# RMSNorm and QKV projection on one core: the last 256 columns as one matmul group, copied in halves by two engines, stored once

One core of one Trainium2 chip. The metric is the time of one execution in microseconds (us) on that core, lower is better; most executions of one kernel agree within about 0.3%. TensorE does the matmuls, VectorE (DVE in the profile) and ScalarE (ACT) copy results out of PSUM (the buffer into which TensorE writes), SyncE (SP) issues the stores. A store has landed when it has signalled its semaphore, a counter that other engines can wait for.

## The reference

```python
def setup_inputs():
    batch, n_heads, seq, head_dim = 8, 12, 1024, 64
    dim = n_heads * head_dim                                   # 768
    return {"x": randn(batch, seq, dim), "gamma": ones(dim),
            "w_qkv": randn(dim, 3 * dim) * 0.1, "eps": 1e-5}   # float32

def reference(x, gamma, w_qkv, eps):
    rms = np.sqrt(np.mean(x ** 2, axis=-1, keepdims=True) + eps)
    x_norm = x / rms * gamma
    return np.matmul(x_norm, w_qkv).astype(np.float32)
```

That is a matmul of 8192 x 768 by 768 x 2304. The kernel works in 64 row tiles of 128 rows; a row tile's 2304 output columns are made in groups (512, 512, 512, 512, 256), each of six accumulating bf16 matmuls into one PSUM tile.

## The kernel before

Only the last row tile (t = MT - 1 = 63) matters here. Its last 256 columns are two groups of 128, each in a PSUM tile of its own.

```python
def width(t, n0):
    return P if t == MT - 1 and n0 >= N - 2 * P else min(NT, N - n0)

def mm(t, n0, kos):
    nl = width(t, n0)
    for ko in kos:
        if (t, n0) not in PM:
            PM[t, n0] = psum.tile([P, NT], f32, name="pm")
        ...
        nc.tensor.matmul(out=PM[t, n0][:, :nl], lhsT=XT[t][:, ko, :], rhs=w_b[:, ko, n0:n0 + nl], ...)

def evac(t, n0, eng):
    ...
    if eng == "DVE":
        nc.vector.tensor_scalar(out=o, in0=pm[:, :nl], scalar1=RS[t], scalar2=None, op0=mult)
    else:
        nc.scalar.activation(out=o, in_=pm[:, :nl], func=AF.Copy, scale=RS[t], bias=0.0)

def store(t, h, n0, nl):
    nc.sync.dma_start(out=of[t * P:(t + 1) * P, n0:n0 + nl], in_=OUT[t, h][...])

def evac_at(time, t, n0, eng, gap):
    at(time, evac, t, n0, eng)
    ...
    if t >= MT - 2:                       # the last two row tiles: each group is stored by itself
        at(time + gap - 0.5, store, t, h, n0, nl)
    elif left[t, h] == 0:
        at(time + gap, store, t, h, *PARTS[h])
...
for t in range(HEAD, MT):
    ...                                   # engines alternate from group to group
    for n0 in [*range(0, N, NT)] + [N - P] * (t == MT - 1):
        at(now, mm, t, n0, range(KO))
        now += width(t, n0) * US
        flip ^= 1
        evac_at(now + 0.2, t, n0, "DVE" if flip else "ACT", gap=1.2)
```

Of the kernel before, what the change touches and what calls it, by code (L numbers as in the profile page):

```python
# [92 lines left out]
def kernel(  # L93
# [8 lines left out]
    nc = tc.nc  # L102
    f32 = mybir.dt.float32
    bf16 = mybir.dt.bfloat16
    AF = mybir.ActivationFunctionType
    mult = mybir.AluOpType.mult
# [4 lines left out]
    Kw, N = w_qkv.shape  # L111
    assert K == Kw
    P = 128
    KO = K // P
    MT = M // P
    NT = 512
# [34 lines left out]
    X, XB, XT, RS, OUT, WF, PM, PT = {}, {}, {}, {}, {}, {}, {}, {}  # L151
# [71 lines left out]
    begun = {}  # L223

    def width(t, n0):

        return P if t == MT - 1 and n0 >= N - 2 * P else min(NT, N - n0)

    def mm(t, n0, kos):
        nl = width(t, n0)  # L230
# [3 lines that stand above are left out]
            b = begun[t, n0] = begun.get((t, n0), 0) + 1  # L234
            nc.tensor.matmul(out=PM[t, n0][:, :nl], lhsT=XT[t][:, ko, :], rhs=w_b[:, ko, n0:n0 + nl],  # L235
                             start=(b == 1), stop=(b == KO))

    def part(n0):
        return max(i for i, (p0, _) in enumerate(PARTS) if p0 <= n0)

    def evac(t, n0, eng):
        nl = width(t, n0)
        h = part(n0)
        if (t, h) not in OUT:
            OUT[t, h] = outp.tile([P, PARTS[h][1]], f32, name=f"ot{h}")
        o = OUT[t, h][:, n0 - PARTS[h][0]:n0 - PARTS[h][0] + nl]
        pm = PM[t, n0]
        if eng == "DVE":
            nc.vector.tensor_scalar(out=o, in0=pm[:, :nl], scalar1=RS[t], scalar2=None, op0=mult)  # L249
        else:  # L250
            nc.scalar.activation(out=o, in_=pm[:, :nl], func=AF.Copy, scale=RS[t], bias=0.0)  # L251

    def store(t, h, n0, nl):
        p0 = PARTS[h][0]
# [6 lines left out]
    def at(time, fn, *args):  # L261
        plan.append((time, len(plan), fn, args))
# [8 lines left out]
    def evac_at(time, t, n0, eng, gap):  # L271
        at(time, evac, t, n0, eng)
        h = part(n0)
        nl = width(t, n0)
        left[t, h] = left.get((t, h), PARTS[h][1]) - nl
        if t >= MT - 2:
# [3 lines that stand above are left out]
# [27 lines left out]
    for t in range(HEAD, MT):  # L307

        ahead = 6.0 if t < HEAD + 5 else 0.0
        if ("x", t) not in {q[1:] for q in LOADS}:  # L310
            at(now - 15 - ahead, load_x, t)
        at(now - 8.5 - ahead, cast, t)
        at(now - 7.5 - ahead, xbar, t)
        at(now - 5, stat, t)
        at(now - 3, recip, t)
        for n0 in [*range(0, N, NT)] + [N - P] * (t == MT - 1):
            at(now, mm, t, n0, range(KO))
            now += width(t, n0) * US
            flip ^= 1
            evac_at(now + 0.2, t, n0, "DVE" if flip else "ACT", gap=1.2)  # L320
# [38 lines left out]
```

## Time and profile before

| | |
|---|---|
| time, median of 3 | 388.26 us (388.1 to 388.3) |
| span of the profiled execution | 386.86 us |
| start of the copy of the last 512-column group | 382.565 us |
| last landing of a store | 385.857 us |

The page gives busy time by engine, the chain of waits that ended last, and groups of instructions by source line. The timeline gives single instructions: start, length, engine, line, operation, output<-input, count, and in brackets the idle time before and what ended it. SPq lines are SyncE issuing transfers; an issue is over long before its data have landed.

**T is the start of the copy of columns 1536 to 2047 of the last tile** (VectorE, 128x512). The change alters no engine's instructions before TensorE's last group, whose first matmul starts 0.20 us before T.

### The profile page before, as it was taken

Reading aid. Unit: us, or ns where it says so; the run is one execution under the profiler, and the core shown is the slowest. Engines: PE = TensorE matmul, PEld = TensorE weight load, DVE = VectorE, ACT = ScalarE, POOL = GpSimd, SP = SyncE. Lnnn points to the kernel's source line nnn. Section 1 sums busy time; section 2 is a strip of 40 time slices with the busy share of each in tenths; the row PEclk is TensorE's granted clock in tenths of the full one; section 3 lists DMA queues with packets and bytes.
Section 4 is the critical chain, followed back from the end, with each engine's and each line's share of the span. In section 5 each row is a group of like instructions: output and inputs, shape, how many; then the busy total and the mean of one; then the engine's idle time right before and its main releaser. Section 6 shows DMA issues by size and latency. Waiting matters only on the chain.

```text
span 386.9 us, 5470 instructions
## 1 busy us (share of the span) xinstructions
PE 379.9 (98%) x1927; PEld 192.2 (50%) x1965; DVE 153.4 (40%) x307; ACT 181.6 (47%) x365; POOL 6.5 (2%) x14
## 2 busy tenths in 40 slices
PE   8999999999999999999999999999999999999996
PEld 4444655454554554554554554554554554554553
DVE  2744534434333344333344333343333343333332
ACT  4752644453544443544444444544444534434532
POOL 0130000000000000000000000000000000000000
PEclk9999999999999999999999999999999999999999
DMA  8999999999999999999999999999999999999985
GB/s 291 390 281 402 398 318 363 344 338 283 351 297 308 303 295 321 293 300 322 305 289 313 285 318 312 293 309 275 326 311 297 304 317 305 304 306 289 292 264 186
DMA packets 89719, 119.91 MB, mean 310 GB/s; under 512 B 52438, under 2 KB 61532, under 8 KB 89692
## 3 DMA queue, kind: packets, MB, share of 16 engines
q1 hardware_dynamic: 89680, 119.56, 101.2%
q8 instruction: 15, 0.25, 0.3%
q14 instruction: 12, 0.10, 0.1%
q10 hardware_dynamic: 12, 0.00, 0.0%
HBM read 32.25 MB, written 75.50 MB: 279 GB/s over the span
## 4 chain that ended last, share of the span: by engine, by line
PE 89%; DMA 8%; issue 1%; DVE 1%; ACT 1%; SPq 0%
PE pm L235 89%; DMA x_t<-in_x_dram 3%; DMA w_f<-in_w_qkv_dram 2%; DMA xT<-xb 2%; DMA out_dram<-ot 1%; ACT ot L251 1%; DVE ot L249 0%; DVE xb L174 0%; SPq L160 0%; SPq L155 0%; SPq L255 0%; ACT w_b L168 0%
## 5 line engine op out<-in xcount | busy, mean ns | idle before, releaser
L235 PE MATMUL pm<-w_b,xT 128*128 128x512 bf16 (+1 forms) x1888 | 372.1, 357 | 2.1
L235 PEld LDWEIGHTS <-xT 128*128 128x128 bf16 x1926 | 187.9, 98 | 185.5 <-DMA xT<-xb 0.5
L249 DVE TENSOR_SCALAR ot<-pm,rstd 128x512 f32<-128x512 f32 (+1 forms) x161 | 111.5, 695 | 206.1 <-PE pm L235 201.7
L251 ACT ACTIVATE ot<-pm,rstd 128x512 f32<-128x512 f32 (+2 forms) x160 | 102.7, 643 | 191.7 <-PE pm L235 151.0
L185 ACT ACTIVATE sq<-x_t 128x768 bf16<-128x768 f32 x64 | 53.4, 834 | 3.0 <-DMA x_t<-in_x_dram 3.0
L174 DVE CAST xb<-x_t 128x768 bf16<-128x768 f32 x61 | 33.2, 545 | 13.6 <-DMA x_t<-in_x_dram 13.5
L187 ACT ACTIVATE rms<-ssq,eps_sb 128x1 f32<-128x1 f32 x64 | 18.8, 294 | 2.1
L185 ACT ACTIVATION_READ_ACCUMULATOR sq<-x_t 128x1 f32 x64 | 12.2, 191 | 0.0
L166 DVE TENSOR_SCALAR w_b<-w_f,g_sb 128x512 bf16<-128x512 f32 (+1 forms) x16 | 7.7, 499 | 5.9 <-DMA w_f<-in_w_qkv_dram 5.9
L192 DVE RECIPROCAL rstd<-rms 128x1 f32<-128x1 f32 x64 | 9.8, 153 | 0.0
L170 POOL TENSOR_SCALAR w_b<-w_f,g_sb 128x512 bf16<-128x512 f32 (+1 forms) x8 | 5.8, 735 | 23.5 <-DMA w_f<-in_w_qkv_dram 23.5
L284 PE MATMUL pm<-const-bfloat16-1.0 128*128 128x512 bf16 (+1 forms) x14 | 5.4, 539 | 0.8 <-PEq L340 0.8
L168 ACT ACTIVATE w_b<-w_f,g_sb 128x512 bf16<-128x512 f32 (+1 forms) x6 | 3.6, 612 | 2.7 <-DMA w_f<-in_w_qkv_dram 2.7
L212 PE MATMUL pm<-ident_f,x_t 128*128 128x128 f32 x18 | 2.8, 300 | 0.3 <-DMA x_t<-in_x_dram 0.3
L212 PEld LDWEIGHTS pm<-ident_f,x_t 128*128 128x128 f32 x18 | 2.4, 160 | 1.3 <-DMA x_t<-in_x_dram 0.9
L284 PEld LDWEIGHTS <-const-bfloat16-1.0 128*128 128x128 bf16 x14 | 1.5, 126 | 2.7 <-issue 2.7
L176 ACT CAST xT<-pm 128x256 bf16<-128x256 f32 (+1 forms) x5 | 2.3, 458 | 0.9 <-PE pm L212 0.7
L142 ACT ACT_TABLE_LOAD x1 | 1.3, 1283 | 1.4 <-PEq L340 1.4
L174 DVE CAST xT<-pm 128x512 bf16<-128x512 f32 x1 | 0.7, 691 | 1.4 <-PE pm L212 1.4
L267 DVE COPY g_sb<-pm 128x6 f32<-128x6 f32 x1 | 0.2, 164 | 1.9 <-PE pm L266 1.9
L266 PEld LDWEIGHTS pm<-ident_f,g 6*128 6x128 f32 x1 | 0.2, 177 | 1.0 <-issue 1.0
L174 DVE COPY xT<-pm 128x768 bf16<-128x768 bf16 x1 | 0.6, 557 | 0.0
(12 smaller groups left out, 2.5 us busy)
## 6 DMA issues: line engine op xcount, KB each, us to landing
out_dram<-ot SPq DMA_DIRECT2D x124, 512.0 KB, 3.9
x_t<-in_x_dram SPq DMA_DIRECT2D x64, 384.0 KB, 4.2
out_dram<-ot SPq DMA_DIRECT2D x63, 128.0 KB, 3.2
w_f<-in_w_qkv_dram SPq DMA_DIRECT2D x10, 512.0 KB, 7.4
out_dram<-ot SPq DMA_DIRECT2D x8, 256.0 KB, 2.0
w_f<-in_w_qkv_dram SPq DMA_DIRECT2D x4, 256.0 KB, 6.6
xT<-xb SPq DMA_TRANSPOSE x60, 4.3
w_f<-in_w_qkv_dram SPq DMA_DIRECT2D x2, 384.0 KB, 6.1
```

The source lines that it names most:

```text
L166: nc.vector.tensor_scalar(out=o, in0=i, scalar1=g, scalar2=None, op0=mult)
L168: nc.scalar.activation(out=o, in_=i, func=AF.Copy, scale=g, bias=0.0)
L170: nc.gpsimd.tensor_scalar(out=o, in0=i, scalar1=g, scalar2=1.0, op0=mult, op1=mult)
L174: nc.vector.tensor_copy(out=out, in_=in_)
L185: nc.scalar.activation(out=sq, in_=X[t], func=AF.Square, accum_out=ssq)
L187: nc.scalar.activation(out=rms, in_=ssq, func=AF.Sqrt, scale=inv_k, bias=eps_sb)
L192: nc.vector.reciprocal(out=r, in_=RS[t])
L212: nc.tensor.transpose(out=PT[t, h][:, ko - k0, :], in_=X[t][:, ko * P:(ko + 1) * P], identity=ident_f)
L235: nc.tensor.matmul(out=PM[t, n0][:, :nl], lhsT=XT[t][:, ko, :], rhs=w_b[:, ko, n0:n0 + nl], start=(b == 1), stop=(b == KO))
L249: nc.vector.tensor_scalar(out=o, in0=pm[:, :nl], scalar1=RS[t], scalar2=None, op0=mult)
L251: nc.scalar.activation(out=o, in_=pm[:, :nl], func=AF.Copy, scale=RS[t], bias=0.0)
L284: nc.tensor.matmul(out=wps[:, :nl], lhsT=ones[:, :P], rhs=ones[:, :nl], start=True, stop=True)
```

## The change

The intent: fewer, larger matmuls at the end, one store issue less, and the longer copy shared by two engines at once.

```diff
     def width(t, n0):
-        return P if t == MT - 1 and n0 >= N - 2 * P else min(NT, N - n0)
+        return min(NT, N - n0)
...
-        if eng == "DVE":
-            nc.vector.tensor_scalar(out=o, in0=pm[:, :nl], scalar1=RS[t], scalar2=None, op0=mult)
-        else:
-            nc.scalar.activation(out=o, in_=pm[:, :nl], func=AF.Copy, scale=RS[t], bias=0.0)
+        both = t == MT - 1 and n0 + nl == N
+        d = nl if eng == "DVE" and not both else P if both else 0
+        if d:
+            nc.vector.tensor_scalar(out=o[:, :d], in0=pm[:, :d], scalar1=RS[t], scalar2=None, op0=mult)
+        if d < nl:
+            nc.scalar.activation(out=o[:, d:], in_=pm[:, d:nl], func=AF.Copy, scale=RS[t], bias=0.0)
...
-        for n0 in [*range(0, N, NT)] + [N - P] * (t == MT - 1):
+        for n0 in range(0, N, NT):
```

The single store follows from the single group.

## The prediction

> **What bounds the kernel now.** I read the page first (busy shares, slices), then the chain that ended last, then the last five microseconds instruction by instruction, since the change touches only the last row tile's last 256 columns.
>
> The page:
>
> ```profile
> span 386.9 us, 5470 instructions
> PE 379.9 (98%) x1927; PEld 192.2 (50%) x1965; DVE 153.4 (40%) x307; ACT 181.6 (47%) x365; POOL 6.5 (2%) x14
> PEclk9999999999999999999999999999999999999999
> PE 89%; DMA 8%; issue 1%; DVE 1%; ACT 1%; SPq 0%
> L235 PE MATMUL pm<-w_b,xT 128*128 128x512 bf16 (+1 forms) x1888 | 372.1, 357 | 2.1
> ```
>
> TensorE is busy for 98% of the span at full clock, with 2.1 us of idle time before 1888 matmuls: everything up to the last matmul is bound by TensorE's matmuls. A change of copies or stores can move the end only by what happens after TensorE stops. (The 357 ns is a pipelined matmul's latency, not its pitch.) The chain names stores as releasers of some copies near the end, with waits of 1.8 to 2.1 us; I discount that, because those copies start at 378.68, 379.97, 381.27 and 382.56, one every 1.29 us, which is six 512-column matmuls at 0.215 us. They follow TensorE.
>
> The timeline of the end, asked for in short windows (start, length, what):
>
> ```profile
> 382.56 0.75 DVE L249 TENSOR_SCALAR ot<-pm,rstd 128x512 f32<-128x512 f32 x1 [1.84 <-DMA out_dram<-ot]
> 382.90 0.37 ACT L251 ACTIVATE ot<-pm,rstd 128x128 f32<-128x128 f32 x1 [0.94 <-PE pm L235]
> 383.23 0.35 DVE L249 TENSOR_SCALAR ot<-pm,rstd 128x128 f32<-128x128 f32 x1
> 383.34 0.33 SPq L255 DMA_DIRECT2D out_dram<-ot  x1
> ...
> 383.77 0.88 SPq L255 DMA_DIRECT2D out_dram<-ot  x2
> ...
> 384.24 0.40 SPq L255 DMA_DIRECT2D out_dram<-ot  x1
> ```
>
> The last 512-column group is copied from 382.56, the first 128-column group from 382.90 (ScalarE), the second from 383.23 (VectorE, done 383.58). SyncE then issues three stores: 256 KB at 383.34, 64 KB at 383.77, 64 KB at 384.24. The last waits not for its data, ready at 383.58, but for SyncE: an issue takes 0.33 to 0.40 us, and 0.09 us pass before the next. So the last store leaves 0.66 us late, and that is what the change can win back.
>
> How long stores take to land, and the final wait (views of the DMA and of the DMA queue's waits over the end):
>
> ```profile
> out_dram<-ot SPq DMA_DIRECT2D x6, 256.0 KB, 2.0
> out_dram<-ot SPq DMA_DIRECT2D x1, 128.0 KB, 2.2
> out_dram<-ot SPq DMA_DIRECT2D x2, 64.0 KB, 1.6
> ...
> SPq L354 <- DMA out_dram<-ot: 1.1, 1, 1.1
> ```
>
> The last landing is at about 384.24 + 1.6 = 385.85; SyncE waits 1.1 us for it after its last issue, and about 1.0 us of closing follows to 386.86. The change does not touch that last part.
>
> **What the Trainium skill says.** (1) "PSUM — Partial Sum Buffer", section "PSUM bank collisions raise a hardware error": two engines must not touch the same bank and 32-partition quadrant at once, reads against reads and disjoint columns included; the compiler there adds a dependency between any two such instructions. This decides the case. The two new copies read columns 0 to 127 and 128 to 255 of one group, 1 KB per partition of one 2 KB bank, all partitions. In the built program of the changed kernel the ScalarE copy indeed no longer waits for TensorE: it waits for VectorE, whose only newer instruction is the other half. The trace of before cannot show this, as no bank there has two copiers. (2) "TensorE: Matmul & The Clock Gate", "Back-to-back issue gap": alone, a warm matmul costs N/2.4 + 2.5 ns, but 81 ns at N=128 in a stream with weight loads. The trace agrees with the first: 0.33 us for six 128-column matmuls (382.90 to 383.23) is 56 ns each, not 81. (3) "DMA: Bandwidth & Descriptors", "Anatomy of one DMA": a transfer has a large fixed part, mostly the write receipt, and a part for its bytes. The page's 2.0 us fixed part is for the software path; here 64 KB land in 1.6 us and 256 KB in 2.0, which leaves about 1.5 us fixed.
>
> **The change part by part.** Each instruction sequence before the last group is the same in the built programs. At the end:
>
> Matmuls: twelve 128-column ones become six of 256, on the path. Before, 382.56 to 383.23 is 0.67 us. The preceding row tile's 256-column group took 377.38 - 376.73 = 0.65 us by the starts of its copies. So the group is ready at 382.56 + 0.65 = 383.21; gain 0.02. Fewer weight loads win nothing, as they are hidden now.
>
> Copies: before, the second 128-column copy alone followed the last matmul, 0.35 us. Now VectorE's half runs 383.21 to 383.56, then, some 0.04 us of signalling later (estimate, from the 0.03 between a copy's end and its store's start), ScalarE's half, 0.37 us, to 383.97. On the path: 0.35 becomes about 0.76, a loss of 0.41 in readiness of the last data, of which the queue of stores hides all but 0.20: SyncE is free for the second store at 383.77 in either kernel.
>
> Stores: two of 64 KB become one of 128 KB. Before, the last starts at 384.24. Now it starts at 383.97 + 0.03 = 384.00, gain 0.24. One issue with its spacing (0.47 us) is gone, and the serial copies eat half of it.
>
> Landing: 128 KB take longer than 64 KB. Interpolating 1.6 (64 KB) and 2.0 (256 KB) by bytes gives 1.73 us, a loss of 0.13. The measured 2.2 for 128 KB fell beside an instruction fetch (an 8 KB packet of the instruction queue in that window), so I don't use it. A check on bandwidth: in the table of 0.1 us stretches, data of the 256 KB store flow from 384.15 to about 384.85 at 370 to 450 GB/s, then the two stores of 512-byte rows at 180 to 270 GB/s to 385.45. A store issued at 384.00 would have its data start at 384.83 (0.83 after issue, as for the one of 383.34), just behind the 256 KB; 128 KB in 1 KB rows at some 300 to 380 GB/s (estimate between the two rates) need 0.34 to 0.44 us, to 385.17 to 385.3, so 0.15 to 0.3 earlier. The two estimates bracket 0.1 to 0.3.
>
> Sum: matmuls and copies and issue together 384.24 to 384.00, -0.24; landing +0.13; net -0.11 to -0.12, so landing at 385.73 and a span of 386.75. In the timed runs 388.26 - 0.12 = 388.14; leaning a little to the bandwidth estimate, 388.1. That is 0.03% of the time.
>
> **The rivals.** (a) The halves really run at once: ScalarE starts at 383.21 too and ends 383.58, the store leaves at 383.77 as soon as SyncE is free, 0.47 earlier; but its data then queue behind the 256 KB store, so landing is some 0.25 to 0.35 earlier: 388.0. Against it speaks the wait for VectorE in the built program. (b) The landing time swallows the gain: if a 128 KB store takes 1.85 us or more (1.6 plus the 0.24 gained), or its issue is held up as the 128 KB one of the preceding tile was (started 378.19, 0.32 after its copy ended at 377.87), the time is unchanged or 0.1 to 0.3 worse: 388.3 to 388.5. For it speak the 2.2 us in the one quiet example; against it the instruction fetch beside it. (c) The two-state noise or a shift in early loads moves more than the tail does: nothing early is changed, and the three runs differ by 0.2 us, so I allow about that much.
>
> **Range and chances.** The mechanism gives -0.35 to +0.2 around 388.26; with the spread of runs and of chips, 387.8 to 388.5. A 2% move would be 7.8 us; the whole time after TensorE's last matmul is 3.6 us, so the change cannot give it, and only a disturbed run could. Faster and slower each 0.007, same 0.986.
>
> **What would show it right or wrong.** ScalarE's 128-column copy starting at about 383.6, after VectorE's has ended, shows the serial copies; at 383.2 it shows rival (a). The last store's start at about 384.0 confirms the issue step; 383.77 means the copies did not matter; 384.3 would mean a delay at SyncE. Landing 1.7 us after it confirms the size step. TensorE's end within 0.03 us of 383.2 confirms the matmul step. The prediction falls if anything before 382 moves by over 0.2 us, or if the closing microsecond changes.

## The result, and the profile after

The change ran in 388.24 us (median of 6 runs, 387.92 to 389.13) against 388.21 us (median of 6, 387.88 to 388.62) for the kernel before. The ratio is the mean time of one kernel's fast runs over that of the other's of the same rounds, so not quite the ratio of the medians: 1.0004, 95% interval 0.9992 to 1.0017. By the clock nothing happened. The trace says more. The page of the change:

```profile
span 387.4 us, 5456 instructions
PE 379.7 (98%) x1921; PEld 191.6 (49%) x1959; DVE 153.2 (40%) x307; ACT 181.5 (47%) x365; POOL 6.5 (2%) x14
```

The profiled span is 0.5 us longer than before's. That has nothing to do with the change: T is already 0.75 us later (383.318 against 382.565). The chain of waits from the start shows most of that in the first loads; first before, then the change (start, length, what):

```profile
1.75 5.58 DMA x_t<-in_x_dram
```

```profile
1.75 6.17 DMA x_t<-in_x_dram
```

Those loads are the same in both kernels, and in a later trace of the changed kernel (run h) T is 382.406. Over the traces T lies anywhere from 382.03 to 383.32 us. That scatter of over a microsecond at the start buries the end, where the change acts. From T on, the trace of the change ends after 4.04 us and that of before after 4.29: the end did get shorter, by 0.25 us, 0.07% of the time. The timeline of the change, in short windows:

```profile
383.32 0.75 DVE L251 TENSOR_SCALAR ot<-pm,rstd 128x512 f32<-128x512 f32 x1 [1.84 <-DMA out_dram<-ot]
...
383.98 0.34 DVE L251 TENSOR_SCALAR ot<-pm,rstd 128x128 f32<-128x128 f32 x1
384.10 0.33 SPq L257 DMA_DIRECT2D out_dram<-ot  x1
...
384.36 0.37 ACT L253 ACTIVATE ot<-pm,rstd 128x128 f32<-128x128 f32 x1 [1.65 <-DVE ot L251]
...
384.75 0.33 SPq L257 DMA_DIRECT2D out_dram<-ot  x1
```

ScalarE's half starts at 384.36, 0.03 us after VectorE's ended (383.984 + 0.343 = 384.327), and the bracket names VectorE as what released it. The halves were not copied at once. The output tile that they share does not explain this: before's last two copies write into one output tile too, from two PSUM tiles, and there VectorE's starts at T+0.669, before ScalarE's ends at T+0.700, and waits for TensorE alone. What is new is the shared PSUM tile. The store leaves at T+1.44; before's last one left at T+1.68.

Two more things differ at the end. The rate at which the last data flow, in stretches of 0.2 us from T+2.23 on (the last two columns are the share of the 16 DMA engines and GB/s); before, then the change:

```profile
384.80:385.00 0.20, 0.00 (x0) 0.00 (x0) 0.00 (x0) 0.00 (x0) 0.00 (x0) 1.00 0.79 251
385.00:385.20 0.20, 0.00 (x0) 0.00 (x0) 0.00 (x0) 0.00 (x0) 0.00 (x0) 1.00 0.78 223
385.20:385.40 0.20, 0.00 (x0) 0.00 (x0) 0.00 (x0) 0.00 (x0) 0.00 (x0) 1.00 0.88 261
385.40:385.60 0.20, 0.00 (x0) 0.00 (x0) 0.00 (x0) 0.00 (x0) 0.00 (x0) 0.62 0.13 33
```

```profile
385.55:385.75 0.20, 0.00 (x0) 0.00 (x0) 0.00 (x0) 0.00 (x0) 0.00 (x0) 1.00 0.92 323
385.75:385.95 0.20, 0.00 (x0) 0.00 (x0) 0.00 (x0) 0.00 (x0) 0.00 (x0) 1.00 1.01 348
385.95:386.15 0.20, 0.00 (x0) 0.00 (x0) 0.00 (x0) 0.00 (x0) 0.00 (x0) 1.00 0.40 128
```

The end of the 256 KB store, until T+2.45 in both, and the last 128 KB move at 320 to 350 GB/s in place of 220 to 260. The change's transfers go on without a pause until the data run out. Before's nearly pause once, near T+2.6, as shorter stretches of its trace show:

```profile
385.00:385.10 0.10, 0.00 (x0) 0.00 (x0) 0.00 (x0) 0.00 (x0) 0.00 (x0) 1.00 0.91 267
385.10:385.20 0.10, 0.00 (x0) 0.00 (x0) 0.00 (x0) 0.00 (x0) 0.00 (x0) 1.00 0.64 180
385.20:385.30 0.10, 0.00 (x0) 0.00 (x0) 0.00 (x0) 0.00 (x0) 0.00 (x0) 1.00 0.90 271
```

That is about when the data of before's last store, issued at T+1.68, can begin: the first packet of the 256 KB store came 0.83 us after its issue, which makes T+2.51 (estimate).

And what SyncE does after its last wait for a store: it checks completion semaphores, up to two with one EVENT_SEMAPHORE instruction. The instructions of the program's last line, in the stretch after that wait; before, then the change (count, length in ns, first and last start):

```profile
L354 SPq EVENT_SEMAPHORE  x3: 28/28/28, 385.9 to 386.0; - x3
```

```profile
L356 SPq EVENT_SEMAPHORE  x1: 28/28/28, 386.5 to 386.5; - x1
```

Three checks are left in before, one in the change. In the trace they start 0.064 us apart, and from the last landing to the end of the span before takes 1.00 us and the change 0.87.

### The profile page after: what moved, and what is told of

The parts are those of the page before. It is cut to its first block, busy times and chain, and to the rows that moved or that the text cites. A ratio compares the mean times of both kernels' runs of the same rounds, so it can differ in the third digit from the quotient of the medians.

```text
span 387.4 us, 5456 instructions
## 1 busy us (share of the span) xinstructions
PE 379.7 (98%) x1921; PEld 191.6 (49%) x1959; DVE 153.2 (40%) x307; ACT 181.5 (47%) x365; POOL 6.5 (2%) x14
## 4 chain that ended last, share of the span: by engine, by line
PE 89%; DMA 8%; issue 1%; ACT 1%; DVE 1%; SPq 0%; DVEq 0%
PE pm L234 89%; DMA x_t<-in_x_dram 3%; DMA w_f<-in_w_qkv_dram 2%; DMA xT<-xb 2%; DMA out_dram<-ot 1%; ACT ot L253 1%; DVE ot L251 0%; DVE xb L174 0%; SPq L160 0%; SPq L155 0%; SPq L257 0%; DVEq L356 0%; ACT w_b L168 0%
```

## The experiments

All numbers from T, in us, out of each trace ("data end" is the end of the last packet that carries data, "closing" is from the last landing to the end of the span; f2 and f3 have no such copy, and there T is 1.30 us after the start of ScalarE's copy of columns 1024 to 1535, as in before):

| kernel | last store leaves | data end | last landing | closing | end |
|---|---|---|---|---|---|
| before | 1.68 | 2.94 | 3.29 | 1.00 | 4.29 |
| the change | 1.44 | 2.82 | 3.16 | 0.87 | 4.04 |
| the change again (h) | 1.44 | 2.82 | 3.17 | 0.87 | 4.04 |
| one copy by ScalarE (e1) | 1.20 | 2.82 | 3.17 | 0.94 | 4.11 |
| before, one store (e2) | 1.21 | 2.81 | 3.15 | 0.94 | 4.09 |
| the change, two stores (e3) | 1.68 | 2.93 | 3.28 | 0.94 | 4.22 |
| the change, other semaphore (e4) | 1.44 | 2.82 | 3.16 | 1.08 | 4.24 |
| e1, two stores by rows (g2) | 1.80 | 3.50 | 3.85 | 1.00 | 4.85 |
| before, ScalarE issues its store (g4) | 1.20 | 2.89 | 3.32 | 1.00 | 4.32 |
| the change, 512-byte pieces (g5) | 1.44 | 2.92 | 3.27 | 0.87 | 4.14 |
| three groups of 256 (f2) | 1.18 | 2.52 | 2.87 | 0.83 | 3.70 |
| f2 with a last pair of 128 (f3) | 1.08 | 2.43 | 2.78 | 0.83 | 3.62 |

All gave correct results. Runs with one execution have no known state; their places after T are still comparable, since TensorE's granted clock was 0.999 or 1.0 in each. My theory at this point was that of the prediction: the end is set by when the last store is issued. The rival was that it is set by data already queued.

**e1: the split copy taken out.** One ScalarE copy of all 256 columns.

```diff
-        both = t == MT - 1 and n0 + nl == N
+        both = False
```

> The change without its splitting of the copy: one matmul group of 256 columns, one ScalarE copy of all 256, one 128 KB store. Let T be the start of VectorE's copy of the last 512-column group; before ended at T+4.29 us and the change at T+4.04. My theory (the halves run one after the other, so the split only delays the store): ScalarE copies from T+0.67 to T+1.14, SyncE is free at T+1.20 and the store starts there, 0.23 earlier than with the halves; landing between T+2.93 (1.73 after issue) and T+3.0 (queued behind the 256 KB store); end at T+3.87 to T+3.95. Rival (the split helps, or the end hangs on the data of the 256 KB store alone): the store starts at T+1.44 or later, or it lands at T+3.16 all the same, and the end is at T+4.04 or later. In the whole time 0.1 to 0.2 us, below the scatter of the runs.

The timeline of e1 around its copy, T being 383.218, and then its SyncE queue's final wait for a store (total, times, longest, in us):

```profile
383.87 0.47 ACT L253 ACTIVATE ot<-pm,rstd 128x256 f32<-128x256 f32 x1 [1.26 <-PE pm L234]
384.00 0.33 SPq L257 DMA_DIRECT2D out_dram<-ot  x1
...
384.42 0.38 SPq L257 DMA_DIRECT2D out_dram<-ot  x1
```

```profile
SPq L356 <- DMA out_dram<-ot: 1.4, 1, 1.4
```

One copy of 256 columns takes 0.47 us, the two serial halves took 0.74, so the store leaves 0.23 us earlier, as I expected. It then lands at T+3.17, as with the change: SyncE merely waits longer, 1.4 us (1.2 in the same view of the change). My theory fell and the rival held. The data end at T+2.82 in either. In time: 388.31 us against 388.37, ratio 0.9994, interval 0.9978 to 1.0011.

**e2: the store alone.** Before's groups and copies, with one store.

```diff
-        if t >= MT - 2:
+        if t == MT - 1 and n0 >= N - 2 * P:
+            if n0 == N - P:
+                at(time + gap - 0.5, store, t, h, N - 2 * P, 2 * P)
+        elif t >= MT - 2:
             at(time + gap - 0.5, store, t, h, n0, nl)
```

> The kernel before with only its last two stores of 64 KB made one of 128 KB: two matmul groups of 128 columns in two banks, each copied by its own engine. Theory (the gain of the change is the saved store issue, not the merged matmuls or the split copy): copies ready at T+1.02, store at T+1.20 when SyncE is free, landing T+2.93 to T+3.0, end T+3.87 to T+3.95, better than the whole change at T+4.04. Rival (the merged matmul group is what gained): end near T+4.29 as before.

The store left at T+1.21 and landed at T+3.15, end T+4.09. The end was later than I expected, for the reason seen in e1, but the question is answered: the landing gain of 0.13 to 0.14 us comes with the single store alone; neither the merged matmul group nor the two-engine copy is needed for it.

**e3: two stores again.** The change, with its store cut in two by columns.

```diff
-            at(time + gap - 0.5, store, t, h, n0, nl)
+            for q in range(n0, n0 + nl, P if t == MT - 1 and n0 + nl == N else nl):
+                at(time + gap - 0.5, store, t, h, q, P if t == MT - 1 and n0 + nl == N else nl)
```

> The change with its one store made two of 64 KB again: merged matmul group, halves copied one after the other. Theory: the first store leaves at T+1.20, the second at T+1.68 when SyncE is free, as in before, so the serial copies are hidden; last landing at T+3.29 as before; end T+4.23 with a closing of 0.94. Rival (one store is not what matters): end T+4.04 as with the change.

Landing T+3.28, end T+4.22, as expected. With two stores the gain in landing is gone, so the merged matmuls and the serial copies are worth nothing for it by themselves. The 0.07 us left at the end are closing, 0.94 in place of 1.00.

**e4: another semaphore for the last store.** The stores signal eight semaphores in turn. Three more stores far from the end move the last one to another semaphore.

```diff
-            at(time + gap, store, t, h, *PARTS[h])
+            if t in (28, 30, 32) and h == 2:
+                at(time + gap, store, t, h, N - 2 * P, P)
+                at(time + gap, store, t, h, N - P, P)
+            else:
+                at(time + gap, store, t, h, *PARTS[h])
```

> The change, with three 128 KB stores of early row tiles split into two of 64 KB each, far from the end: the DMA completion semaphores are used in turn, eight of them, so the last store now signals another one. SyncE waits for all eight at the end in a fixed order, about 0.064 us each; what it still has to check after the last landing is added to the end. Before had three checks left after it and a closing of 1.00 us, the change one left and 0.87. Here the last store's semaphore is checked first, four are left. Theory: store at T+1.44 and landing at T+3.16 as with the change, closing 1.06 to 1.07, end T+4.23. Rival (the shorter closing came from something else in the change, such as one instruction less or one store less): closing stays 0.87, end T+4.04.

Store and landing stayed at T+1.44 and T+3.16, and the closing grew from 0.87 to 1.08 us, a little over the 1.06 to 1.07 expected. So 0.13 of the change's 0.25 us is an accident. In the built programs, one store less turns the rotation, and VectorE's own count drops out of the list as ScalarE has waited for it; one check is left behind the last store's in place of three. e1, e2 and e3, with two left, lie between at 0.94.

**g2: as many stores, longer rows.** e1 with the last 128 KB cut by rows.

```diff
+        if t == MT - 1 and n0 + nl == N:
+            for q in (0, 64):
+                nc.sync.dma_start(out=of[t * P + q:t * P + q + 64, n0:n0 + nl],
+                                  in_=OUT[t, h][q:q + 64, n0 - p0:n0 - p0 + nl])
+            return
         nc.sync.dma_start(out=of[t * P:(t + 1) * P, n0:n0 + nl], in_=OUT[t, h][...])
```

> One matmul group and one ScalarE copy of 256 columns, but the last 128 KB as two stores of 64 KB, split by rows: 64 partitions by 256 columns each, so as many stores as in before, with 1 KB rows in place of 512-byte rows. The first three experiments showed a landing at T+3.15 to T+3.17 with one store of 128 KB whether it left at T+1.20 or at T+1.44, and T+3.28 to T+3.29 with two stores of 128 columns. Theory A (the data of the last 384 KB are the bound; 512-byte rows move slower): second store leaves at T+1.64 to T+1.68 and lands at T+3.14 to T+3.20, end T+4.14 to T+4.20 with a closing of 1.00. Theory B (the last issue sets the landing, as I predicted at first): it lands 1.61 after its issue, at T+3.25 to T+3.29, end T+4.25 to T+4.29.

Neither theory: the issues of these 64-partition stores took 0.55 and 0.58 us in place of 0.33 to 0.40, the last left at T+1.80 and landed at T+3.85. The cut changed something other than what it was meant to change, so the run decides nothing between the two. Why such a store is slower to issue stays open.

**g4: the last store issued earlier, same rows.** Before, with one of its last two stores issued by ScalarE.

```diff
-        nc.sync.dma_start(out=...
+        q = nc.scalar if t == MT - 1 and n0 == N - 2 * P else nc.sync
+        q.dma_start(out=...
```

> The kernel before with one edit: the store of ScalarE's last 128 columns is issued by ScalarE itself, at about T+0.73, so SyncE's store of VectorE's 128 columns leaves at about T+1.20 in place of T+1.68. Same matmuls, copies, bytes and 512-byte rows as before. Theory A (the last 384 KB flow without a pause and 512-byte rows move slower than 1 KB rows, so the landing doesn't depend on the last issue): last landing stays at T+3.2 to T+3.3 and the data end at T+2.85 to T+2.94. Theory B (the issue at T+1.68 sets the landing): the last landing comes at T+3.15 or earlier, as with one store of 128 KB.

The issues in the timeline of g4 (ACTq is ScalarE's sequencer):

```profile
382.76 0.40 ACTq L256 DMA_DIRECT2D out_dram<-ot  x1
382.81 0.81 SPq L256 DMA_DIRECT2D out_dram<-ot  x2
```

T is 382.032: ScalarE issues at T+0.73 and SyncE's two issues now end at T+1.59. The last issue is 0.48 us earlier than in before, and the near pause is gone, as the stretches from T+2.50 on show:

```profile
384.53:384.63 0.10, 0.00 (x0) 0.00 (x0) 0.00 (x0) 0.00 (x0) 0.00 (x0) 1.00 0.83 246
384.63:384.73 0.10, 0.00 (x0) 0.00 (x0) 0.00 (x0) 0.00 (x0) 0.00 (x0) 1.00 0.88 267
```

The data end 0.05 us earlier, at T+2.89. So in before the queue at SyncE did cost something, but about 0.05 us by this one run, and not the whole wait. The last landing doesn't even come earlier, at T+3.32 against T+3.29 and 0.02 past the range of Theory A: it follows 0.43 us after the data, where it is about 0.35 in all the other runs. Why is open; ScalarE's store runs on a DMA queue of its own here, its packets from T+1.77 to T+2.68 among those of the 256 KB store. Theory B's landing at T+3.15 or earlier is out.

**g5: one store, short pieces.** The change, its halves copied into a tile with a gap between them, so that the one store moves pieces of 512 bytes.

```diff
+        if t == MT - 1 and h == 2:
+            OUT[t, h] = outp.tile([P, 2, P + 64], f32, name="otg", bufs=1)
+            ... # VectorE copies into [:, 0, :P], ScalarE into [:, 1, :P]
...
+            nc.sync.dma_start(out=of[...].rearrange("p (q c) -> p q c", q=2), in_=OUT[t, h][:, :, :P])
```

> The change with one edit: the two halves are copied into a tile with a gap between them, so the one store of 128 KB, at T+1.44 as in the change, has to move 256 pieces of 512 bytes in place of 128 pieces of 1 KB. What the runs left open is whether the earlier landing comes from longer rows or from one transfer less. Theory rows: 512-byte packets show in the trace, the data end at T+2.9 to T+2.95 and the landing comes at T+3.25 to T+3.32, end T+4.12 to T+4.2 with a closing of 0.87. Theory transfers: landing at T+3.16 as with the change, end T+4.04.

The rates at the end of g5, in the columns shown above:

```profile
385.54:385.74 0.20, 0.00 (x0) 0.00 (x0) 0.00 (x0) 0.00 (x0) 0.00 (x0) 1.00 0.77 256
385.74:385.94 0.20, 0.00 (x0) 0.00 (x0) 0.00 (x0) 0.00 (x0) 0.00 (x0) 1.00 0.96 292
385.94:386.14 0.20, 0.00 (x0) 0.00 (x0) 0.00 (x0) 0.00 (x0) 0.00 (x0) 1.00 0.87 266
```

One store, issued when the change's was, but with 256 packets of 512 bytes in place of 128 of 1 KB. The rates, from T+2.24, fall to 260 to 290 GB/s and the landing moves from T+3.16 to T+3.27. So with one store in both, the pieces alone change the landing. How much of that is their size itself is not settled. A packet of 512 bytes takes its DMA engine 26.5 ns on average in g5, one of 1 KB 47 ns in the change, so 256 of the first take 16 engines 0.42 us and 128 of the second 0.38 (estimates from these means), which explains some 0.05 of the 0.11 us. But g5 also began later: the issue of its store took 0.38 us in place of 0.33, and the first packet came at T+2.35 in place of T+2.29. From the other side, g4 has 512-byte pieces and no near pause, and its data end 0.07 us after the change's. The gain of 0.12 us at the end of the data is thus about 0.05 from the near pause that went and 0.07 from the longer pieces and the one store less (estimates from one trace each).

**f2 and f3: a version built on this.** If the end hangs on data queued behind the last 512-column group's 256 KB, the last groups should be smaller, so that less is queued. f2 makes the last 768 columns as three groups of 256, one copy and one 128 KB store each, and turns the semaphores so that the last store's is checked last (e4's edit, for six stores).

```diff
-        return min(NT, N - n0)
+        return 2 * P if t == MT - 1 and n0 >= 3 * NT else min(NT, N - n0)
...
-        both = t == MT - 1 and n0 + nl == N
+        both = False
...
-        for n0 in range(0, N, NT):
+        for n0 in (0, 512, 1024, 1536, 1792, 2048) if t == MT - 1 else range(0, N, NT):
```

> A version built on theory A: the last 768 columns as three matmul groups of 256, each copied by one engine and stored as 128 KB at once, so that less data is queued when the last group is ready; six early stores split in two, so that the last store's semaphore is the last that SyncE checks. T is 1.30 us after the start of ScalarE's copy of the last tile's columns 1024 to 1535, as in the other runs. Theory A: stores leave at about T-0.14, T+0.50 and T+1.17, the last lands at T+2.75 to T+2.9, closing 0.81, end T+3.56 to T+3.7, against T+4.04 for the change and T+4.29 before. Theory B: landing at T+1.17 + 1.73 = T+2.90, end T+3.7. Rival (a fixed time after the last matmul, or the landing of the other stores in flight, holds the end): landing at T+3.1 or later, end T+3.9 or later. In the whole time -0.5 to -0.7 us against before, 0.15%, at the edge of what five rounds resolve.

The last store left at T+1.18 and landed at T+2.87, closing 0.83, end T+3.70: 0.59 us earlier than before. The data rate over the end of f2, in 40 slices of 0.09 us from 382.3 us on:

```profile
GB/s 0 0 0 0 155 354 399 376 376 399 421 310 288 343 343 332 233 332 387 332 244 45 0 89 321 376 343 233 56 0 0 0 0 0 0 0 0 0 0 0
```

The rate now falls to zero before the last store's data: the queue runs dry, and the landing, 1.69 us after the issue, is set by the issue again. Both theories gave nearly the same number here, so this run supports the use of the finding, not the finding. In time: 387.77 us (median of 6) against 388.44 (median of 11), ratio 0.998, interval 0.9966 to 0.9993.

f3 cuts the last 256 columns into two groups of 128 again and lets ScalarE issue the very last store (five early stores are split, for the same semaphore).

```diff
-        return 2 * P if t == MT - 1 and n0 >= 3 * NT else min(NT, N - n0)
+        return (P if n0 >= 4 * NT else 2 * P) if t == MT - 1 and n0 >= 3 * NT else min(NT, N - n0)
...
+        q = nc.scalar if t == MT - 1 and n0 + nl == N else nc.sync
```

> As the last, but the last 256 columns again as two groups of 128 with one copy and one 64 KB store each, and the very last store issued by ScalarE itself after its copy, so that it doesn't wait for SyncE. Theory: the last store leaves at T+1.06 and lands at T+2.5 to T+2.75, end T+3.3 to T+3.55. Rival (512-byte rows and the extra store cost what the earlier issue gains): landing at T+2.8 or later, end T+3.6 or later, no better than three groups of 256.

Landing T+2.78, between the theory and the rival, and end T+3.62, in the rival's range, though 0.08 us ahead of f2: 0.10 us were gained at the issue and 0.08 of them kept; the data of the last two 64 KB stores follow the one before without a pause again. In time 387.76 us against 388.44, ratio 0.9977, interval 0.9963 to 0.9991, not to be told from f2. Both intervals lie below 1, so both versions are faster than before, by some 0.2%. The traces account for 0.6 to 0.7 us of it, 0.15 to 0.17%.

**h: the change once more,** unedited, as a control.

> The change itself once more, unedited, as a control: its end should be at T+4.03 to T+4.05 in the trace again, if differences of 0.05 us there are to mean anything; in the timed runs a ratio to before within 0.2% of 1, its true gain of about 0.25 us (0.07%) being smaller than the scatter of single runs of some 0.5 us.

End at T+4.041 against T+4.037: the end repeats to 0.004 us. In time 387.97 us (median of 5) against 388.33 (median of 9), ratio 0.9989, interval 0.9975 to 1.0003. The first measurement's median was 0.03 us above before's, this one's 0.36 below, for one and the same kernel; the gain of 0.25 us in the traces is below what such a number of runs resolves.

## Why the prediction was right or wrong

The time, 388.24 us, lies in the range of 387.8 to 388.5, near the 388.1 predicted, and within 2% as expected. That tests little, as the runs of one kernel scatter by more than any step of the prediction. Point by point, from the traces:

- **TensorE bounds everything to the last matmul; only the end can change.** Right. The merged matmuls were to make the last group ready 0.02 us earlier; TensorE's last matmul ends at T+0.616 in the change against T+0.631 in before (ends are modelled), and e1's copy starts as much earlier, T+0.654 against T+0.669. The change kept little of that: VectorE, with no idle time after its copy of 512 columns, starts its half at T+0.666.
- **The halves run one after the other.** Right (the trace shows the wait that was expected; no run shows what happens without it): predicted 383.60 after VectorE's end at 383.56, against T = 382.56; that is T+1.04, and ScalarE started at T+1.04. Rival (a) is out; its landing of 0.25 to 0.35 us earlier was too much as well, as e2's store left at T+1.21 and landed 0.14 us earlier. e1 shows that one engine alone is quicker than the two in turn, 0.47 against 0.74 us.
- **The last store leaves 0.24 us earlier.** Right: T+1.68 to T+1.44.
- **What the earlier issue wins back.** Wrong. I read the last store, ready but waiting for SyncE, as 0.66 us "that the change can win back", and added the landing times to the issues. e1 (issued 0.23 earlier still, same landing) and g4 (before's last issue 0.48 earlier, data end 0.05 earlier, landing 0.03 later) show that at most some 0.05 us of that wait reached the end. The data of the preceding 256 KB store flow until T+2.45, and in the change the last 128 KB follow at once; what changed besides is how fast they flow, 1 KB pieces against 512-byte ones (g5).
- **Landing 0.11 to 0.12 us earlier net.** Right in size (0.13 measured, T+3.29 to T+3.16). The sum of issue and landing, 1.73 us after issue, even matched to 0.01, but by chance: in e1 the same store takes 1.97 us. The side check by bandwidth in the prediction, 0.15 to 0.3 us earlier, was nearer to the mechanism, and I had used it as a check only. It came out too early since it had the data of the 256 KB store end at 384.85, that is T+2.29; they end at T+2.45.
- **The closing microsecond is not touched.** Wrong: 1.00 to 0.87 us, half of the gain in the trace. I listed a changed closing as what would make the prediction fall. By that sign it did fall here, though the whole time doesn't show it, as 0.13 us is small beside the scatter. e4 shows the cause.
- **The spread.** Too small. I took 0.2 us from three runs; the runs of one kernel, where it was timed five times or more, spread over 0.4 to 1.8 us, and in the traces that scatter arises before T. The prediction was also to fall if anything before 382 moved by over 0.2 us. T moved by 0.75, but between two traces of the changed kernel alone it moves by 0.91, so that sign was no test of the change.

## What to carry to other kernels

A store that was ready and waited 0.66 us for its issuing engine cost some 0.05 us here, as the data before it were still flowing most of that time; before shortening an issue queue, look whether the transfers pause. Two engines copying different columns of one PSUM group took turns here, 0.74 us against 0.47 for one engine alone, so look in the trace whether a split copy runs at once before counting on it; a split across two PSUM banks was not tried. For a change at the very end, read the trace from a mark just ahead of it: the end repeated to 0.004 us there, while the whole time scattered by more than the effect.

## What the Trainium skill lacked or had wrong

- "DMA: Bandwidth & Descriptors", section "Specifications", gives 512 bytes as the least size for full rate. Here 128 KB stored in 512-byte pieces moved at 260 to 290 GB/s (g5) and in 1 KB pieces at 320 to 350 (the change).
- "TensorE: Matmul & The Clock Gate", section "Back-to-back issue gap", gives 81 ns for a 128-column matmul in a stream with weight loads; the runs show 56 ns, its figure for one alone.
- No page that I looked up tells that each check of semaphores which SyncE still has to make after the last landing costs about 0.064 us. From the last landing to the end of the span it was 0.83 to 1.08 us, so the place of the last store in the rotation of semaphores is worth up to 0.25 us.
- No page that I looked up tells that a store of 64 partitions is slower to issue than one of 128: 0.55 and 0.58 us against 0.33 to 0.40 (g2, one run).
